# Model-wide activations stored 320 words per row instead of 322, and MLP inner chunks begun at shifted addresses

## The chip, the cores and the metric

The kernel runs on one core of a Trainium2 chip. The metric is the time of one execution in device microseconds (us), as the median of the runs shown. The core's engines are named as the profile names them: PE is TensorE, which multiplies; PEld is the same engine's weight load; DVE is VectorE, ACT is ScalarE, POOL is GpSimd and SP is SyncE, which here only issues transfers. SBUF is the on-chip memory of 128 partitions in which operands lie; PSUM is the memory into which TensorE writes.

## The reference, cut to what matters

One inference step of a two-layer decoder over 320 tokens (256 of a prompt, 8 sequences of 8 new tokens), model width 2048, all in float32:

```python
# layer 0: gated linear attention; layer 1: chunked spatial gating; after each a dense MLP
h = mixer(x)                                           # x @ w_in, the mixer itself, ... @ w_out
x = layer_norm(ALPHA * x + h)
x = layer_norm(ALPHA * x + square(relu(x @ w1)) @ w2)  # w1: 2048 x 8192, w2: 8192 x 2048
```

Nearly all of the arithmetic is the products with the weights: w_in and w_out of both mixers, w1 and w2 of both layers.

## The kernel before

**Layout.** Activations lie transposed: features on the 128 partitions, tokens on the free axis. A model-wide activation has 2048 features, so it is 16 "k rows" of 320 tokens side by side in each partition. The kernel keeps every such activation as two float32r tiles, a high part and a low part, whose sum is the float32 value; the weights are split in the same way as they arrive. Four buffers hold all these activations in turn: a0 and a1 (high and low), b0 and b1. Each has 16 rows of TW = 322 words: 320 tokens, and two columns that are used only where a layer norm's gain and offset ride along in the product. So row k begins 1288 * k bytes behind the start of its buffer. As the program is built, the buffers begin at byte 18976 (a0), 39584 (a1), 60192 (b0) and 150176 (b1) of a partition, which is 32, 160, 32 and 160 modulo 256.

**Products.** `group` (L143) works out two feature tiles of 128 outputs. It fetches the weights in units of 4 k rows by 256 columns (`unit`, L117: the transfer is issued by SP at L127, ACT rounds to the high part at L128, DVE takes the low part at L129), and for each k row and each of the two output tiles `mm3` (L136) issues three matmuls of 320 columns: low weights by high activation (L139), high weights by low activation (L140), high by high (L141). In the names of the profile `mm<-hh,wl` is: into the PSUM tile mm, moving operand hh (the activation), stationary operand wl (the weights). The activation's name is x (input), o (mixer output of layer 0), dg (an unnormed activation times the gain, with the two extra columns: 322 wide), y (normed), h (inner chunk of the MLP) or p (mixer output of layer 1), followed by h or l for its part. The weight units rotate through rings of SBUF tiles; in a partition all tiles of one ring begin at 160 modulo 256 (ring a, the only one during the heads), all tiles of the other at 224 (ring b).

```python
    def mm3(ps, wh, wl, kk, n, rh, rl, k, c0, cn, first, last):
        s = slice(n * P, (n + 1) * P)
        x_h, x_l = rh[:, k, c0 : c0 + cn], rl[:, k, c0 : c0 + cn]
        nc.tensor.matmul(ps, wl[:, kk, s], x_h, start=first, stop=False)
        nc.tensor.matmul(ps, wh[:, kk, s], x_l, start=False, stop=False)
        nc.tensor.matmul(ps, wh[:, kk, s], x_h, start=False, stop=last)
...
    def bigtile(tag, dt, name):
        return (lp if tag == "b1" else big).tile([P, KT, TW], dt, tag=tag, name=nm(name))

    def parts(pair, name):
        return bigtile(pair + "0", F32R, name + "h"), bigtile(pair + "1", F32R, name + "l")
```

**Stages.** In order of time: the four heads of layer 0 (products with x, in buffers a, between which small matmuls of the attention run); the output product with o (buffers a); the MLP of layer 0, whose y lies in a and whose inner chunks h lie in b: for each of four chunks c of 2048 inner features `mlp` (L774) makes h = square(relu(y @ w1)) and adds h @ w2 to the residual z; then layer 1: y in b for the spatial gating, p in b, and the second MLP with y in b and h in a. The first two pairs of output tiles after a norm run on dg instead of y (`gemm_of`, L741). The last layer norm ends the program. There are 736 weight units, so 17,664 matmuls of the lines L139 to L141, of which 576 are 322 columns wide and the rest 320.

**What sets the order.** Each engine runs its own stream in the order in which the program was built; transfers of weights are issued ahead as ring tiles come free.

Of the kernel before, what the change touches and what calls it, by code (L numbers as in the profile page):

```python
# [15 lines left out]
P = 128  # L16
D = 2048
KT = D // P          # feature tiles of a model-width activation
TP = 256             # prompt tokens
DB, DS = 8, 8        # sample batch and new tokens  # L20
T = TP + DB * DS     # tokens side by side on the free axis
TW = T + 2           # with two columns for the gain and the offset of a norm
H = 4
DK, DV = 256, 512
CH = 64              # GLA chunk
# [5 lines left out]
UK = 4               # k tiles in a weight unit  # L31
UN = 256             # columns in a weight unit
NU = KT // UK

# columns of the per-feature vectors
# [6 lines left out]
class Ring:  # L42
    """Where the split weight units of a GEMM live."""
# [5 lines left out]
class Side:  # L49
    """Work beside a GEMM, handed out in steps over the weight units still to come."""  # L50
# [16 lines left out]
def step_kernel(ctx: ExitStack, tc: tile.TileContext, A):  # L67
# [7 lines left out]
    # ------------------------------------------------------------ pools  # L75
# [13 lines left out]

    def mmtile(n=T):  # L90
        """Of the banks for products; two more of them once the heads are done."""
        if mx is not None:
            banks[0] = (banks[0] + 1) % 6
        return (mx if banks[0] > 3 else mm).tile([P, n], F32, tag="mm", name=nm("mm"), padded_shape=[P, 512])
# [4 lines left out]
    # ------------------------------------------------------------ constants  # L99
# [16 lines left out]
    # ------------------------------------------------------------ weights  # L116
    def unit(w, row0, q, col0, ring):  # L117
        """UK k tiles of UN columns, as exact high and low parts."""
        raw = wraw.tile([P, UK, UN], F32, tag="raw", name=nm("raw"))
        src = w[row0 // (UK * P) + q, col0 // UN]  # L120
        hi = ring.pool.tile([P, UK, UN], F32R, tag="h" + ring.tag, name=nm("wh"))
        lo = ring.pool.tile([P, UK, UN], F32R, tag="l" + ring.tag, name=nm("wl"))
        units[0] += 1
        step = 2 if units[0] <= 2 else UK  # the first ones in parts, for an early start
        for k in range(0, UK, step):
            ks = slice(k, k + step)
            nc.sync.dma_start(raw[:, ks, :], src[:, ks, :])  # L127
            nc.scalar.copy(hi[:, ks, :], raw[:, ks, :])  # L128
            nc.vector.tensor_sub(lo[:, ks, :], raw[:, ks, :], hi[:, ks, :].bitcast(F32))  # L129
        return hi, lo  # L130
# [11 lines left out]

    def group(w, row0, cols, rh, rl, evict, side=None, width=T, before=None):  # L143
        """Two feature tiles of w[row0:row0+D].T @ x for each of cols, k tiles outermost in units."""
        ps = [mmtile(width) for _ in range(2 * len(cols))]
        for q in range(NU):
            if before is not None:
                before(q)
            for i, c in enumerate(cols):
                wh, wl = unit(w, row0, q, c, next_ring())  # L150
                for n in range(2):
                    for kk in range(UK):
                        k = q * UK + kk
                        mm3(ps[2 * i + n][:], wh, wl, kk, n, rh, rl, k, 0, width, k == 0, k == KT - 1)
                if side is not None:
                    side()
        for n in range(2 * len(cols)):
            evict(n, ps[n])

    def rsqrt(out, src, scale, eps, eps_t, pool):  # L160
        """1 / sqrt(scale * src + eps): the table's value and a Newton step."""
# [10 lines left out]
    # ------------------------------------------------------------ layer 0: GLA  # L172
# [3 lines left out]
    def bigtile(tag, dt, name):  # L176
        """A model-wide activation in one of four buffers; b1 comes with the later pool."""
        return (lp if tag == "b1" else big).tile([P, KT, TW], dt, tag=tag, name=nm(name))

    def parts(pair, name):  # L180
        return bigtile(pair + "0", F32R, name + "h"), bigtile(pair + "1", F32R, name + "l")
# [9 lines left out]
    # x, by k tiles, and its parts  # L191
    xT = A["xT"].rearrange("(k p) t -> p k t", p=P)
    def load_x(q):
        """x for quarter q of the features."""
# [12 lines left out]
    # causal masks: prompt [s of a 128-block, (t | t of the second block)]; sample [(i, part, s), (i', t)]  # L207
# [20 lines left out]
    # where the masked scores and the sample's queries go; what they leave is zero  # L228
# [9 lines left out]
    # per head: [1, d1, d1 d2 | 1, d2] for the queries, [d1 d2 d3, d2 d3, d3, 1] for the keys  # L238
# [8 lines left out]
    def load_gates():  # L247
        """The gate's weights; the second ones by 32 rows: high parts (twice), low parts."""
# [7 lines left out]
    def low_gate():  # L256
        """rows 0-15 x @ w_hi, rows 16-31 x @ w_lo, [hi | lo] side by side in the stationary operand; three times"""
# [22 lines left out]
    def bc4(ap):  # L280
        """[P, 64] sample columns -> [P, 8, 4, 8], the same for each part."""
        return ap.rearrange("p (b o t) -> p b o t", b=DB, o=1)
# [4 lines left out]
    class Head:  # L287
        """The gates of a head, its k, q and v, and what GLA reads of them."""
# [16 lines left out]
        def gate_logits(hd):  # L305
            """exp(-|z|) and min(z, 0) of the logits z; a step for each table of ScalarE."""
# [12 lines left out]
        def gate_sums(hd):  # L319
            """log_sigmoid(z) = min(z, 0) - ln(1 + exp(-|z|)), summed along the chunks."""  # L320
# [93 lines left out]
        def project_kq(hd, side, before=None):  # L414
            """k and q together, as all four tiles of the other heads' work beside it are there."""
# [25 lines left out]
        def weigh(hd):  # L441
            """o * g * silu(r)"""
# [5 lines left out]
        def finish(hd):  # L448
            """... over the root of the mean square"""
# [4 lines left out]
        def prompt_scores(hd):  # L454
            """Scores of all chunk pairs at once, [s, t] for each block of 128 keys."""
# [64 lines left out]
        def sample_first(hd):  # L520
            """rows: 64 of the queries' high parts, 64 of the low ones"""
# [7 lines left out]
        def sample_step(hd, b, kt):  # L529
            """What state tile (b, kt) adds to o, and its update."""  # L530
# [39 lines left out]
        def steps(hd):  # L570
            """GLA, by steps: the prompt at once, the sample's sequences one by one."""
# [22 lines left out]
    # ------------------------------------------------------------ the rest: residual stream z  # L594
# [7 lines left out]
    def second_half():  # L602
        """The heads are done: their tiles make room for the residual stream."""
# [16 lines left out]
    class Norm:  # L620
        """LayerNorm over the features of src, of sums of d = src - c, c[t] the mean of the first half.

        The GEMM that reads it starts on d * g: with the columns g and offset beside it, its rows are
        put right by mean and 1/std as they leave.
        """

        def __init__(self, src, vg, vb, raw=None, last=False):
# [5 lines left out]
            if raw is not None:  # L633
                self.raw = gh, gl_ = parts(raw, "dg")
# [12 lines left out]
        def total(self, x):  # L647
            """Sums over the partitions, of x in its two parts."""
# [9 lines left out]
        def take(self, j):  # L658
            """The shifted tile j into the sums; where nothing follows, the last one straight into the totals."""
# [19 lines left out]
        def add(self, j):  # L679
            """Tile j is there; of the second half already shifted."""  # L680
# [9 lines left out]
            else:  # L690
                # any c does, as long as it is the same everywhere
# [9 lines left out]
        def close(self):  # L701
            """The mean (negative) and 1/std."""
# [8 lines left out]
        def apply(self, j, yh=None, yl=None):  # L711
            """In place (x - mean) * rstd * g + b of one feature tile, and its parts."""
# [10 lines left out]
        def correct(self, ps):  # L723
            """From a row tile of w.T @ [d * g | g | b]: the product with the norm, less its offset, and that."""
# [7 lines left out]
    def gemm(w, row0, col0, rh, rl, evict, quad=False, side=None, before=None):  # L732
        """All feature tiles, in pairs; the first two pairs together where x is only coming."""
# [7 lines left out]
    def gemm_of(norm, out, w, col0, evict_raw, evict):  # L741
        """w.T @ norm(x): its first tiles from d * g while the norm itself is worked out."""
        yh, yl = parts(out, "y")
# [8 lines left out]
    def residual_gemm(w, rh, rl, row0, scale, vg, vb, raw, quad=False, side=None, before=None, last=False):  # L752
        """z <- scale * z + x @ w, shifted, with the sums for its norm along with the evictions."""
# [20 lines left out]
    def mlp(i, norm, y_in, h_in, vg, vb, raw, last=False):  # L774
        """z, normed, and its MLP; z and the sums for the norm of what comes out."""
        w1, w2 = A["mlp_w1"][i], A["mlp_w2"][i]
        NC_ = 4
        for c in range(NC_):
            hs = []

            def sq_relu(j, x, r):
                if not hs:
                    hs.extend(parts(h_in, "h"))
# [17 lines left out]
            if c == 0:  # L801
                yh, yl = gemm_of(norm, y_in, w1, 0, evict_raw, evict)
# [9 lines left out]
    # layer 0: mixer output, norm, MLP, norm; the last head is still at work beside the first product  # L812
# [10 lines left out]
    # ------------------------------------------------------------ layer 1: spatial gating  # L823
    nv = v = wsT = bb = wss = u_st = None

    def spatial():
        """Causal spatial weights, transposed: [s, g, t]; of the sample the first rows, block-diagonal."""
        nonlocal wsT, bb, wss, u_st
        bsp = bigtile("a1", F32, "bsp")
        bs = bsp[:].rearrange("p k t -> p (k t)")  # L830
# [38 lines left out]
    def mix(j):  # L869
        """The normed feature tile j, mixed over its tokens."""  # L870
# [15 lines left out]
    def mixed(j, pm, g):  # L886
        """... with the bias; in v once its rows are out."""
# [33 lines left out]
    # the last norm, over three engines: d - mean on TensorE from the parts of both, or all of it on GpSimd  # L921
# [101 lines left out]
```

## Time and profile before

| | |
|---|---|
| median of 3 runs | 2784.06 us (2784.03 to 2784.24) |
| profiled execution, from its first to its last instruction (span) | 2783.4 us |
| TensorE: matmul busy, weight load busy | 2763.0 us (99%), 2714.9 us (98%) |
| VectorE, ScalarE, GpSimd busy | 1543.0 us (55%), 1179.7 us (42%), 52.6 us (2%) |
| matmuls recorded | 18,493 |

The span is that of one execution; the median stands 0.7 us above it. Busy time of TensorE counts matmuls that overlap (each is pipelined behind the one before), so 99% says that it nearly always has one under way, not that it could not be quicker.

### The profile page before, as it was taken

The page shows a single profiled execution, that of the slowest core. Times are in us where ns is not written, and L with a number is a line of the kernel's source. Part 1 is how long each engine was busy: PE and PEld are TensorE (multiplying, and loading weights), DVE is VectorE, ACT ScalarE, POOL GpSimd, SP SyncE. Part 2 cuts the span into 40 slices and gives each one's busy share as a digit, 9 for nine tenths or more (in the row PEclk, how much of TensorE's full clock was granted, in tenths as well). Part 3 has the DMA queues.
Part 4 walks back from the last instruction along what each step waited for, and adds up shares of the span by engine and source line. Part 5 has one row for each costly group of instructions (what it writes and reads, how often), then busy time and mean ns, then how long its engine had stood idle before and what let it go on. Part 6 is the DMA issues. An engine that isn't in the chain of part 4 may idle for free.

```text
span 2783.4 us, 44616 instructions
## 1 busy us (share of the span) xinstructions
PE 2763.0 (99%) x18493; PEld 2714.9 (98%) x18493; DVE 1543.0 (55%) x2276; ACT 1179.7 (42%) x1698; POOL 52.6 (2%) x83
## 2 busy tenths in 40 slices
PE   8999999999999999999999999999999999999998
PEld 8898998999999999999999999999999999999998
DVE  6566566886444444444468764587444444444446
ACT  5545454555334324323435553455324323423433
POOL 1000000000000000000000000000000000000001
PEclk9999999999999999999999999999999999999999
DMA  6556565654444445444445444445444444444442
GB/s 221 167 190 227 152 212 190 208 156 152 148 149 152 147 149 151 147 149 151 148 137 175 149 136 126 148 144 152 150 147 151 150 147 151 150 146 151 150 147 75
DMA packets 126396, 434.52 MB, mean 156 GB/s; under 512 B 13681, under 2 KB 17905, under 8 KB 126193
## 3 DMA queue, kind: packets, MB, share of 16 engines
q1 hardware_dynamic: 118800, 407.29, 47.3%
q0 software_dynamic: 6512, 23.20, 2.4%
q8 instruction: 144, 2.36, 0.3%
q10 hardware_dynamic: 880, 1.18, 0.1%
q14 instruction: 60, 0.48, 0.1%
HBM read 409.60 MB, written 22.02 MB: 155 GB/s over the span
## 4 chain that ended last, share of the span: by engine, by line
PE 98%; DVE 0%; ACT 0%; DMA 0%; issue 0%; SPq 0%; ACTq 0%; DVEq 0%
PE mm L139 31%; PE mm L141 31%; PE mm L140 31%; PE gl L540 1%; PE gl L543 1%; PE gl L498 1%; DMA xr<-xT 0%; PE gl L882 0%; PE gl L482 0%; PE gl L883 0%; ACT z L956 0%; DMA raw<-gla_w_in 0%; PE gl L874 0%; PE gl L483 0%; PE gl L409 0%
## 5 line engine op out<-in xcount | busy, mean ns | idle before, releaser
L129 DVE TENSOR_TENSOR wl<-raw,wh 128x1024 fp32r<-128x1024 f32 (+1 forms) x738 | 900.5, 1221 | 991.5 <-ACT wh L128 988.9
L128 ACT CAST wh<-raw 128x1024 fp32r<-128x1024 f32 (+1 forms) x738 | 771.4, 1046 | 1258.3 <-PE mm L141 1140.6
L141 PE MATMUL mm<-yh,wh 128*128 128x320 f32 x2368 | 734.0, 310 | 0.0
L140 PE MATMUL mm<-yl,wh 128*128 128x320 f32 x2368 | 732.4, 310 | 0.0
L139 PE MATMUL mm<-yh,wl 128*128 128x320 f32 x2368 | 727.8, 310 | 0.0
L141 PE MATMUL mm<-hh,wh 128*128 128x320 f32 x2048 | 635.3, 310 | 0.0
L139 PE MATMUL mm<-hh,wl 128*128 128x320 f32 x2048 | 634.4, 310 | 0.0
L140 PE MATMUL mm<-hl,wh 128*128 128x320 f32 x2048 | 633.6, 309 | 0.0
L140 PEld LDWEIGHTS mm<-yl,wh 128*128 128x128 f32 x2368 | 447.0, 189 | 0.2
L141 PEld LDWEIGHTS mm<-yh,wh 128*128 128x128 f32 x2368 | 446.1, 188 | 0.1
L139 PEld LDWEIGHTS mm<-yh,wl 128*128 128x128 f32 x2368 | 444.5, 188 | 0.0
L140 PEld LDWEIGHTS mm<-hl,wh 128*128 128x128 f32 x2048 | 386.7, 189 | 0.0
L141 PEld LDWEIGHTS mm<-hh,wh 128*128 128x128 f32 x2048 | 385.8, 188 | 0.0
L139 PEld LDWEIGHTS mm<-hh,wl 128*128 128x128 f32 x2048 | 385.8, 188 | 0.0
L139 PE MATMUL mm<-xh,wl 128*128 128x320 f32 x768 | 246.4, 321 | 9.7 <-ACT xh L200 5.8
L140 PE MATMUL mm<-xl,wh 128*128 128x320 f32 x768 | 241.1, 314 | 0.2 <-DVE xl L201 0.2
L141 PE MATMUL mm<-xh,wh 128*128 128x320 f32 x768 | 240.2, 313 | 0.0
L139 PEld LDWEIGHTS mm<-xh,wl 128*128 128x128 f32 x768 | 145.7, 190 | 22.1 <-issue 10.8
L140 PEld LDWEIGHTS mm<-xl,wh 128*128 128x128 f32 x768 | 146.3, 190 | 2.8 <-issue 1.4
L141 PEld LDWEIGHTS mm<-xh,wh 128*128 128x128 f32 x768 | 146.0, 190 | 2.2 <-issue 1.2
L792 ACT ACTIVATE r<-mm 128x320 f32<-128x320 f32 x120 | 52.6, 439 | 64.5 <-PE mm L141 64.5
L139 PE MATMUL mm<-ph,wl 128*128 128x320 f32 x256 | 78.9, 310 | 1.0 <-ACT ph L915 1.0
(272 smaller groups left out, 2493.5 us busy)
## 6 DMA issues: line engine op xcount, KB each, us to landing
raw<-mlp_w SPq DMA_DIRECT2D x512, 512.0 KB, 3.5
raw<-gla_w_in SPq DMA_DIRECT2D x94, 512.0 KB, 4.1
raw<-sg_w_in SPq DMA_DIRECT2D x64, 512.0 KB, 3.5
st<-state SPq DMA_DIRECT2D x32, 512.0 KB, 3.9
o_state_s<-st POOLq DMA_DIRECT2D x32, 512.0 KB, 3.8
raw<-gla_w_out SPq DMA_DIRECT2D x32, 512.0 KB, 4.3
raw<-sg_w_out SPq DMA_DIRECT2D x32, 512.0 KB, 3.6
z<-xT POOLq DMA_DIRECT2D x2, 1280.0 KB, 11.4
```

The lines of the kernel that those rows point to most:

```text
L128: nc.scalar.copy(hi[:, ks, :], raw[:, ks, :])
L129: nc.vector.tensor_sub(lo[:, ks, :], raw[:, ks, :], hi[:, ks, :].bitcast(F32))
L139: nc.tensor.matmul(ps, wl[:, kk, s], x_h, start=first, stop=False)
L140: nc.tensor.matmul(ps, wh[:, kk, s], x_l, start=False, stop=False)
L141: nc.tensor.matmul(ps, wh[:, kk, s], x_h, start=False, stop=last)
L498: nc.tensor.matmul(pu[:], hd.ktp[:, blk, kt * P : (kt + 1) * P], hd.vtp[:, blk, :], start=(blk == 0), stop=(blk == 1))
L540: nc.tensor.matmul(po[:], qm[:, kt, b * P : (b + 1) * P], part[:], start=False, stop=(b == DB - 1 and kt == 1 and part is sth))
L543: nc.tensor.matmul(pu[:], hd.kts[32 * i : 32 * (i + 1), g, kt * P : (kt + 1) * P], hd.vts[32 * i : 32 * (i + 1), g, :], start=True, stop=True)
L792: nc.scalar.activation(r[:], ps[:], AF.Relu)
```

## The change

Each buffer becomes one flat run of 16 * 322 words of the same size at the same place. An activation is now a piece of it with rows of 320 words (1280 bytes, which is 5 * 256), beginning at a start offset in words; only the dg activations and the tile of the spatial weights keep rows of 322. Start offsets are 0 except: the inner chunks h of layer 0 begin at 8 * c words (32 * c bytes) in both buffers; those of layer 1 begin at 0 in the high part's buffer and 8 * c in the low part's; the high part of y of layer 1's MLP begins at word 32 (128 bytes). Besides this the diff only drops comments, which shifts no line of the products (L117 to L158) and moves later ones by a line or two.

```diff
-    def bigtile(tag, dt, name):
-        """A model-wide activation in one of four buffers; b1 comes with the later pool."""
-        return (lp if tag == "b1" else big).tile([P, KT, TW], dt, tag=tag, name=nm(name))
-
-    def parts(pair, name):
-        return bigtile(pair + "0", F32R, name + "h"), bigtile(pair + "1", F32R, name + "l")
+    def bigtile(tag, dt, name, width=T, start=0):
+
+        t = (lp if tag == "b1" else big).tile([P, KT * TW], dt, tag=tag, name=nm(name))
+        return t[:, start : start + KT * width].rearrange("p (k t) -> p k t", t=width)
+
+    def parts(pair, name, width=T, starts=(0, 0)):
+        return (bigtile(pair + "0", F32R, name + "h", width, starts[0]),
+                bigtile(pair + "1", F32R, name + "l", width, starts[1]))
...
-                self.raw = gh, gl_ = parts(raw, "dg")
+                self.raw = gh, gl_ = parts(raw, "dg", TW)
...
-    def gemm_of(norm, out, w, col0, evict_raw, evict):
-        """w.T @ norm(x): its first tiles from d * g while the norm itself is worked out."""
-        yh, yl = parts(out, "y")
+    def gemm_of(norm, out, w, col0, evict_raw, evict, starts=(0, 0)):
+
+        yh, yl = parts(out, "y", starts=starts)
...
-                    hs.extend(parts(h_in, "h"))
+                    hs.extend(parts(h_in, "h", starts=(8 * c, 8 * c) if i == 0 else (0, 8 * c)))
...
-                yh, yl = gemm_of(norm, y_in, w1, 0, evict_raw, evict)
+                yh, yl = gemm_of(norm, y_in, w1, 0, evict_raw, evict, starts=(0, 0) if i == 0 else (32, 0))
...
-        bsp = bigtile("a1", F32, "bsp")
-        bs = bsp[:].rearrange("p k t -> p (k t)")
+        bs = bigtile("a1", F32, "bsp", TW).rearrange("p k t -> p (k t)")
```

As built, every engine has the same instructions in the same order with the same waits, and every tile lies where it lay. What differs is the address at which an activation's rows are written and read, and that 16 instructions at the start (the split of x, two k rows at a time) now write one run of 640 words instead of two of 320.

Where the rows begin, in bytes modulo 256, before and after (matmuls of 320 columns, the high part serving two of three):

| activation | matmuls | before: high, low | after: high, low |
|---|---|---|---|
| x, o, p, y of layer 0's MLP and of the gating, h of chunk 0 of both layers | 9,600 | 32 to 152, 160 to 24, in steps of 8 with k | 32, 160 |
| h of layer 0, chunks 1, 2, 3 | 768 each | the same | 64, 192; 96, 224; 128, 0 |
| y of layer 1's MLP | 2,880 | the same | 160, 160 |
| h of layer 1, chunks 1, 2, 3 | 768 each | the same | 32, 192; 32, 224; 32, 0 |

## Rows read from the trace of the kernel before

**Rows 1.** The page: the span, and busy time, share of the span and instructions of each engine.

```profile
span 2783.4 us, 44616 instructions
...
PE 2763.0 (99%) x18493; PEld 2714.9 (98%) x18493; DVE 1543.0 (55%) x2276; ACT 1179.7 (42%) x1698; POOL 52.6 (2%) x83
```

**Rows 2.** The page: the granted clock of TensorE in 40 slices of the span (tenths of full speed), and the chain of work that ended last, its shares by engine and by line.

```profile
PEclk9999999999999999999999999999999999999999
...
PE 98%; DVE 0%; ACT 0%; DMA 0%; issue 0%; SPq 0%; ACTq 0%; DVEq 0%
PE mm L139 31%; PE mm L141 31%; PE mm L140 31%; PE gl L540 1%; PE gl L543 1%; PE gl L498 1%; DMA xr<-xT 0%; PE gl L882 0%; PE gl L482 0%; PE gl L883 0%; ACT z L956 0%; DMA raw<-gla_w_in 0%; PE gl L874 0%; PE gl L483 0%; PE gl L409 0%
```

**Rows 3.** The waits of TensorE's matmuls: line, what it waited for, us in total, times, longest.

```profile
PE mm L139 <- ACT xh L200: 5.8, 1, 5.8
PE mm L139 <- DVE qd L386: 2.1, 1, 2.1
...
PE mm L140 <- DVE xl L201: 0.2, 1, 0.2
```

**Rows 4.** Busy time by stretches of the span, TensorE alone. [...] The stretches: layer 0's h of chunk 0, y of chunk 1, h of chunk 1; layer 1's h of chunks 0 and 2; the last norm.

```profile
core 0: us, PE busy (x), PEclk, DMA share, GB/s
...
700.50:813.70 113.20, 113.20 (x770) 1.00 0.49 149
813.70:926.90 113.20, 113.20 (x770) 1.00 0.49 149
926.90:1040.20 113.30, 113.30 (x770) 1.00 0.49 149
...
1970.30:2083.60 113.30, 113.30 (x771) 1.00 0.49 149
...
2196.80:2310.00 113.20, 113.20 (x770) 1.00 0.49 149
...
2763.60:2783.40 19.80, 10.54 (x62) 0.94 0.38 133
```

**Rows 5.** The timeline of TensorE in layer 0's MLP, h in buffers b: start in us, duration in us, engine, line, operation. Of each three matmuls of a k row only the first (L139) is shown: k rows 11 of the second output tile, then 12, 13, 14, 15 and 12 of the next unit's tiles.

```profile
738.98 0.31 PE L139 MATMUL mm<-hh,wl 128*128 128x320 f32 x1
...
739.44 0.32 PE L139 MATMUL mm<-hh,wl 128*128 128x320 f32 x1
...
739.89 0.30 PE L139 MATMUL mm<-hh,wl 128*128 128x320 f32 x1
...
740.33 0.31 PE L139 MATMUL mm<-hh,wl 128*128 128x320 f32 x1
...
740.76 0.31 PE L139 MATMUL mm<-hh,wl 128*128 128x320 f32 x1
...
741.21 0.31 PE L139 MATMUL mm<-hh,wl 128*128 128x320 f32 x1
```

**Rows 6.** The same place of a group in layer 1's MLP, h in buffers a (the first row is again k row 11), and the weight load that begins beside that first matmul.

```profile
2008.80 0.31 PE L139 MATMUL mm<-hh,wl 128*128 128x320 f32 x1
2008.80 0.19 PEld L140 LDWEIGHTS mm<-hl,wh 128*128 128x128 f32 x1
...
2009.26 0.32 PE L139 MATMUL mm<-hh,wl 128*128 128x320 f32 x1
...
2009.71 0.30 PE L139 MATMUL mm<-hh,wl 128*128 128x320 f32 x1
...
2010.15 0.31 PE L139 MATMUL mm<-hh,wl 128*128 128x320 f32 x1
```

**Rows 7.** The timeline of TensorE: the first and the last of the matmuls counted in the prediction's averages. By time: first of all 16,774 and of the 8,388 whose row begins on a multiple of 16 bytes (9.66); first of the 8,386 whose row begins 8 bytes past one (10.26); first of the rows at 32 modulo 64, and at 160 modulo 256 (13.15); first at 32 modulo 256 (13.30); first at 0 modulo 64 (17.41); then the last ones: at 160 modulo 256 (2750.82), at 32 modulo 256 (2750.96), at 32 modulo 64 (2758.61), at 0 modulo 64 (2762.18), on a multiple of 16 bytes (2763.05), and of all and 8 bytes past a multiple of 16 (2763.35).

```profile
9.66 0.31 PE L139 MATMUL mm<-xh,wl 128*128 128x320 f32 x1
...
10.26 0.31 PE L139 MATMUL mm<-xh,wl 128*128 128x320 f32 x1
...
13.15 0.31 PE L140 MATMUL mm<-xl,wh 128*128 128x320 f32 x1
...
13.30 0.31 PE L141 MATMUL mm<-xh,wh 128*128 128x320 f32 x1
...
17.41 0.31 PE L140 MATMUL mm<-xl,wh 128*128 128x320 f32 x1
...
2750.82 0.31 PE L140 MATMUL mm<-hl,wh 128*128 128x320 f32 x1
...
2750.96 0.31 PE L141 MATMUL mm<-hh,wh 128*128 128x320 f32 x1
...
2758.61 0.31 PE L141 MATMUL mm<-hh,wh 128*128 128x320 f32 x1
...
2762.18 0.31 PE L141 MATMUL mm<-hh,wh 128*128 128x320 f32 x1
...
2763.05 0.31 PE L141 MATMUL mm<-hh,wh 128*128 128x320 f32 x1
...
2763.35 0.31 PE L140 MATMUL mm<-hl,wh 128*128 128x320 f32 x1
```

**Rows 8.** The split of x by two k rows at a time: duration of one in ns (least, median, most), first and last start, shapes.

```profile
L200 ACT CAST xh<-xr x8: 727/728/732, 5.0 to 19.8; 128x640 fp32r<-128x640 f32 x8
...
L201 DVE TENSOR_TENSOR xl<-xr,xh x8: 819/824/1104, 5.8 to 21.7; 128x640 fp32r<-128x640 f32 x8
```

## The prediction, made before the changed kernel was run

> **What bounds the kernel now.** First the page's busy times: TensorE has a matmul under way for 2763.0 of 2783.4 us, the other engines are far from full [rows 1]. Then the chain that ended last: 98% of it is TensorE, 93% the three product lines L139 to L141 [rows 2], and TensorE's longest wait for another engine is 5.8 us, once, at the start [rows 3]. [...] So the time is the number of matmuls times the time from the start of one to the start of the next; I call this the step. A faster ACT, DVE or transfer would be worth nothing.
>
> Next the step itself. The inner stages of both MLPs have 768 matmuls each, whichever buffers they read and whatever goes on beside them, and each takes 113.2 to 113.3 us [rows 4]: 113.25 / 768 = 147.5 ns. [...]
>
> The timeline shows that the step is not even. From one k row's L139 to the next takes three steps: in [rows 5] 0.46, 0.45, 0.44, 0.43, 0.45 us. In the other layer, other buffers, the same place gives 0.46, 0.45, 0.44 us again [rows 6]. The records have whole nanoseconds, so I averaged steps over all matmuls of 320 columns with a product matmul directly behind and no stall (a step of at most 170 ns): 16,774 of them, mean 147.41 ns, standard deviation 2.9, first and last in [rows 7]. Sorted by line, row start modulo 256 and weight address, outside the heads, the same class repeats to 1.1 ns, while the classes' means run from 141 to 157 ns. The step is therefore set by where a matmul reads, or by its place in the sequence; in this kernel those two go together, as k row 3 always begins at the same bytes modulo 256.
>
> Two sortings speak for the address. By row start modulo 64, the means run from 146.4 to 148.5 ns; worked out for the heads alone (one weight ring, attention matmuls between) and for all the rest, the eight means agree with a correlation of 0.8. And buffers a and b, whose starts agree modulo 256 and in little else, give the same step [rows 4].
>
> **The change part by part.** The order of all engines and the waits stay, so every term is a change of the step.
>
> *Rows 320 words apart.* Before, a product sweeps 16 row starts in steps of 8 bytes and pays their mean. After, all 16 rows begin at the same bytes modulo 256, so a stage pays what its one or two starts cost. Of the 17,088 matmuls of 320 columns, 15,040 then begin at 32 modulo 64: the 9,600 with starts 32 and 160; the second chunk of layer 0 shifted by 64 bytes (768); y of layer 1's MLP (2,880); the high parts of layer 1's chunks 1 to 3 (1,536) and one of their low parts (256). The other 2,048 begin at 0 modulo 64. The trace of before has both: 2,086 matmuls at 32 modulo 64 with a mean of 146.62 ns, 2,096 at 0 modulo 64 with 148.08 ns (first and last of each in [rows 7]). So 15,040 x (146.62 - 147.41) = -11.9 us and 2,048 x (148.08 - 147.41) = +1.4 us: -10.5 us.
>
> A finer sorting, modulo 256, has fewer samples: starts at 32 (always a high part) 148.02 ns over 687 matmuls, at 160 (always a low part) 144.58 ns over 346 [rows 7]. The 9,600 with two high and one low take (2 x 148.02 + 144.58) / 3 = 146.87 ns, -0.54 ns, -5.2 us. If it is the address alone, layer 1's y, all at 160, takes 144.58 ns: 2,880 x -2.83 = -8.2 us; if it is the part, nothing. The remaining 4,608, with their starts priced in the same way, come to +0.6 us. Sum -12.7 us, or -4.5 us without the gain on y. I take -12 us, between the two full sums.
>
> *The shifted starts* are in these sums: chunk 3 of layer 0 (128 and 0) is the dear one, at 0 modulo 64; the others lie near the mean or below.
>
> *Alignment.* All rows after begin on a multiple of 16 bytes, before every second one. In the trace the 8,388 aligned ones have a mean of 147.08 ns and the 8,386 others 147.73 [rows 7].
> [...]
>
> *Weight loads.* The load for the next matmul begins as the matmul begins (2008.80 in both rows of [rows 6]), so both read SBUF at once. [...]
> [...]
>
> *The rest.* The 576 matmuls of 322 columns keep their rows. Writes by ACT and DVE go to other addresses; they are hidden behind 99% of TensorE. The 16 merged instructions of the split of x take 728 and 824 ns at the median [rows 8]; only the first lie ahead of the first products, and if a run of 640 cost or saved a tenth, that would be 0.15 us. The last norm's 19.8 us [rows 4] stay.
>
> The profiled execution's 2783.4 us less 12 us are 2771.4; the median stands 0.7 us above its span, so 2772 us, -0.43%. What a measurement of this kernel can tell from no change is about 0.2%, 5.6 us.
>
> **The bounds.** The unknown is the step where the same row start follows itself 16 times, which before never happens. From the dearest and the cheapest three steps of the timeline, 457 ns (0.46 in [rows 5]) and 436 ns (0.43), a step of one start could be 152.3 or 145.3 ns: 17,088 x +4.9 = +84 us or 17,088 x -2.1 = -36 us, if every stage fell on the same end. There are eight different pairs of starts, the commonest with 56% of the matmuls, so I count half of the upper end at most.
>
> **The rivals.**
> *Faster by more.* If the step's unevenness is a phase between two reads, equal rows let it settle, and it settles where nothing collides: the step of rows at 160, 144.58 ns, for all: 17,088 x -2.83 = -48 us, 2736 us; for half of the stages 2760. For it: classes repeat to 1.1 ns, so the pattern does lock. Against: nothing says that it locks at the good end.
>
> *Slower.* The same mechanism, locked at the bad end. Before, the sweep averages good and bad starts; after, 9,600 matmuls share one pair. If these settle at the 150.20 ns that rows at 128 modulo 256 have now (698 matmuls within the same first and last), they cost 9,600 x 2.79 = +27 us: 2811 us. It decides as soon as their step passes 147.41 + 5.6 us / 9,600 = 148.0 ns, where the high parts at 32 modulo 256 already stand by themselves. Against it: their low parts are the cheapest rows there are.
>
> *No change.* The step depends on the place in the sequence and not on the address, or starts average out over the weights' addresses: 2784 us. For it: place and address can't be parted in this trace, and all stages have one step [rows 4]. Against: the sorting by row start agrees between the heads and the rest.
> [...]
>
> [...]
>
> **How the numbers follow.** The forecast, in which averages by row start carry over, 0.42 (own range 2763 to 2778); faster by more 0.18; slower 0.20; no change 0.12; only the lines 0.08. Faster by over 0.2% is the first two, 0.60; the last two make 0.20 for no difference; slower 0.20. The range leaves out about a tenth at each side: 2740, most of the way to the locked good end, to 2795, halfway to the locked bad one.
>
> **What would show it.** Right: stages of 768 matmuls no longer take one time; those with starts 32 and 160 take 112.8 us (146.9 ns), layer 0's chunk 3 longer than its chunk 1, layer 1's y less than layer 0's; within a stage the three steps of every k row are alike. Wrong if every stage still takes 113.25 us (place, not address), if the stages at 32 and 160 take over 113.7 us (locked badly), or if all fall below 112 us. The dg products, whose rows don't move, must keep their time whatever happens; if they change too, something else did it.

## The result, and the profile after

The changed kernel takes 2770.79 us (median of 4 runs, 2770.2 to 2770.9) against 2784.15 us: a ratio of 0.995, 95% interval 0.9936 to 0.9964. That is 13.4 us or 0.48% faster; forecast were 12 us and 2772 us. Its profiled execution has a span of 2769.1 us, 14.3 us below that of [rows 1]. One run of a kernel further down, the one without shifts, took 3334.01 us at a granted clock of 0.753; no figure below uses it.

The page after, the lines that answer to [rows 1] and [rows 2]: span, busy times, granted clock, the chain by line.

```profile
span 2769.1 us, 44616 instructions
...
PE 2749.8 (99%) x18493; PEld 2701.6 (98%) x18493; DVE 1542.8 (56%) x2276; ACT 1179.4 (43%) x1698; POOL 52.8 (2%) x83
...
PEclk9999999999999999999999999999999999999999
...
PE mm L139 31%; PE mm L141 31%; PE mm L140 31%; PE gl L542 1%; PE gl L545 1%; PE gl L500 1%; DMA xr<-xT 0%; PE gl L883 0%; PE gl L484 0%; PE gl L884 0%; ACT z L957 0%; DMA raw<-gla_w_in 0%; PE gl L875 0%; PE gl L485 0%; PE gl L409 0%
```

Nothing moved but TensorE's own pace: the same instructions, the same granted clock (0.999 of full speed over the span, before and after), the same chain, DVE and ACT busy as long as before. PE is shorter by 13.2 us.

Busy time of TensorE by stages, as in [rows 4] (stretch in us from the span's start, its length, busy us and matmuls that touch it, of which up to two at the edges belong to the neighbours, granted clock as a share of full speed, DMA share, GB/s). The stretches are layer 0's h of chunks 0 to 3, one of the dg products with unmoved rows, then layer 1's h of chunks 1 and 2.

```profile
697.97:810.50 112.53, 112.53 (x770) 1.00 0.50 150
923.04:1035.99 112.95, 112.95 (x771) 1.00 0.48 150
1148.52:1260.95 112.43, 112.43 (x771) 1.00 0.48 150
1373.47:1485.98 112.51, 112.51 (x772) 1.00 0.50 150
...
1485.98:1515.03 29.05, 29.05 (x198) 1.00 0.48 146
...
2186.04:2298.05 112.01, 112.01 (x771) 1.00 0.48 151
2410.68:2523.44 112.76, 112.76 (x771) 1.00 0.49 150
```

Before, all of these h stages took 113.2 to 113.3 us. Now each has its own time, by where its rows begin, and all are shorter. The dg product kept its time (29.04 us in the trace before, from 1493.24 to 1522.28).

The timeline at the place of [rows 5] (k row 11 onwards, the first of each three matmuls):

```profile
736.21 0.31 PE L139 MATMUL mm<-hh,wl 128*128 128x320 f32 x1
...
736.65 0.31 PE L139 MATMUL mm<-hh,wl 128*128 128x320 f32 x1
...
737.09 0.31 PE L139 MATMUL mm<-hh,wl 128*128 128x320 f32 x1
...
737.52 0.31 PE L139 MATMUL mm<-hh,wl 128*128 128x320 f32 x1
...
737.97 0.31 PE L139 MATMUL mm<-hh,wl 128*128 128x320 f32 x1
```

From one k row to the next it is 0.44, 0.44, 0.43, 0.45 us where it was 0.46, 0.45, 0.44, 0.43. Averaged as in the prediction, the step (start of one matmul to the start of the next) is 146.54 ns over 16,765 matmuls, standard deviation 2.0, where it was 147.41 and 2.9. 17,088 x 0.87 = 14.9 us: the step alone accounts for the gain (13.4 us in the medians, 14.3 us in the spans).

### The profile page after: what moved, and what is told of

It reads as the page before. It is cut to its first block, busy times and chain, and to the rows that moved or that the text cites. A ratio compares the mean times of both kernels' runs of the same rounds, so it can differ in the third digit from the quotient of the medians.

```text
span 2769.1 us, 44616 instructions
## 1 busy us (share of the span) xinstructions
PE 2749.8 (99%) x18493; PEld 2701.6 (98%) x18493; DVE 1542.8 (56%) x2276; ACT 1179.4 (43%) x1698; POOL 52.8 (2%) x83
## 4 chain that ended last, share of the span: by engine, by line
PE 98%; ACT 1%; DVE 0%; DMA 0%; issue 0%; SPq 0%; ACTq 0%; DVEq 0%
PE mm L139 31%; PE mm L141 31%; PE mm L140 31%; PE gl L542 1%; PE gl L545 1%; PE gl L500 1%; DMA xr<-xT 0%; PE gl L883 0%; PE gl L484 0%; PE gl L884 0%; ACT z L957 0%; DMA raw<-gla_w_in 0%; PE gl L875 0%; PE gl L485 0%; PE gl L409 0%
## 5 line engine op out<-in xcount | busy, mean ns | idle before, releaser
L141 PE MATMUL mm<-yh,wh 128*128 128x320 f32 x2368 | 731.3, 309 | 0.0
L140 PE MATMUL mm<-yl,wh 128*128 128x320 f32 x2368 | 728.7, 308 | 0.0
L139 PE MATMUL mm<-yh,wl 128*128 128x320 f32 x2368 | 724.7, 309 | 0.0
L141 PE MATMUL mm<-hh,wh 128*128 128x320 f32 x2048 | 632.1, 309 | 0.0
L139 PE MATMUL mm<-hh,wl 128*128 128x320 f32 x2048 | 631.8, 308 | 0.0
L140 PE MATMUL mm<-hl,wh 128*128 128x320 f32 x2048 | 631.4, 308 | 0.0
L140 PEld LDWEIGHTS mm<-yl,wh 128*128 128x128 f32 x2368 | 444.7, 188 | 0.2
L141 PEld LDWEIGHTS mm<-yh,wh 128*128 128x128 f32 x2368 | 444.0, 187 | 0.1
L139 PEld LDWEIGHTS mm<-yh,wl 128*128 128x128 f32 x2368 | 443.0, 188 | 0.0
L139 PEld LDWEIGHTS mm<-hh,wl 128*128 128x128 f32 x2048 | 385.0, 188 | 0.0
L140 PEld LDWEIGHTS mm<-hl,wh 128*128 128x128 f32 x2048 | 384.5, 188 | 0.0
L141 PEld LDWEIGHTS mm<-hh,wh 128*128 128x128 f32 x2048 | 384.3, 188 | 0.0
L139 PE MATMUL mm<-xh,wl 128*128 128x320 f32 x768 | 245.7, 320 | 8.6 <-ACT xh L202 5.8
L140 PE MATMUL mm<-xl,wh 128*128 128x320 f32 x768 | 241.3, 314 | 0.2 <-DVE xl L203 0.2
L141 PE MATMUL mm<-xh,wh 128*128 128x320 f32 x768 | 239.7, 312 | 0.0
L139 PEld LDWEIGHTS mm<-xh,wl 128*128 128x128 f32 x768 | 145.8, 190 | 21.2 <-issue 10.9
L140 PEld LDWEIGHTS mm<-xl,wh 128*128 128x128 f32 x768 | 146.1, 190 | 2.8 <-issue 1.4
L141 PEld LDWEIGHTS mm<-xh,wh 128*128 128x128 f32 x768 | 145.9, 190 | 2.3 <-issue 1.2
L139 PE MATMUL mm<-ph,wl 128*128 128x320 f32 x256 | 78.6, 309 | 1.0 <-ACT ph L916 1.0
```

## The experiments

Steps below are such averages over a stage, from the records of its trace. "Pair" means the start offsets of high and low part in words (4 bytes); offset 0 is byte 32 modulo 256 in the high part's buffer and 160 in the low part's, both multiples of 16. "Line" is a name for 16 bytes of a partition that begin at a multiple of 16, not a unit that a trace shows: 320 columns that begin on one lie in 80 of them, those that begin 4, 8 or 12 bytes past one in 81.

**What carries the gain: the shifted starts, equal rows, or whole 16-byte lines?** Three kernels, each against the changed one:

Without any shift, every row of both parts on a whole line:

```diff
-                    hs.extend(parts(h_in, "h", starts=(8 * c, 8 * c) if i == 0 else (0, 8 * c)))
+                    hs.extend(parts(h_in, "h", starts=(0, 0)))
...
-                yh, yl = gemm_of(norm, y_in, w1, 0, evict_raw, evict, starts=(0, 0) if i == 0 else (32, 0))
+                yh, yl = gemm_of(norm, y_in, w1, 0, evict_raw, evict, starts=(0, 0))
```

> All activations keep rows of 320 words, but every start offset is 0, so that every stage reads rows at 32 (high part) and 160 (low part) modulo 256. If the row start alone sets the step, every stage of 768 matmuls now takes the same time, the one that chunk 0 takes in the changed kernel, 112.5 us (146.5 ns a matmul), and the whole is within 3 us of the changed kernel (2771 us). If the shifted starts carried the gain, the time goes back towards 2784 us. If the place in the sequence counted and not the address, the chunks would still differ from each other as they do in the changed kernel (145.8 to 147.1 ns).

Every row 8 bytes past a line (dg keeps its rows): the same two calls with (2, 2), the same default in `gemm_of`, and

```diff
-    def parts(pair, name, width=T, starts=(0, 0)):
+    def parts(pair, name, width=T, starts=(2, 2)):
```

> Rows of 320 words, every start offset 2 words (8 bytes): all rows of the large products begin at 40 and 168 modulo 256, 8 bytes past a multiple of 16, and all rows of a stage still begin at the same bytes. If the gain comes from beginning on a multiple of 16 bytes, it is lost or turned round: a step of 147.7 ns or more, 2789 us. If it comes from all rows beginning alike, whatever the bytes, the step is near 146.5 ns and the time near 2771 us.

Rows of 324 words: the two calls with (0, 0), and

```diff
+TR = T + 4
...
-    def bigtile(tag, dt, name, width=T, start=0):
+    def bigtile(tag, dt, name, width=TR, start=0):
...
-        t = (lp if tag == "b1" else big).tile([P, KT * TW], dt, tag=tag, name=nm(name))
+        t = (lp if tag == "b1" else big).tile([P, KT * TW + 64], dt, tag=tag, name=nm(name))
...
-    def parts(pair, name, width=T, starts=(0, 0)):
+    def parts(pair, name, width=TR, starts=(0, 0)):
```

> Rows of 324 words (1296 bytes), start offset 0, buffers 256 bytes longer so that all of them and the weight rings begin where they did modulo 256. Every row begins on a multiple of 16 bytes, but the 16 rows of a product sweep through 16 different starts again, in steps of 16 bytes. If beginning on a multiple of 16 bytes is what counts, the step is at or below 147.1 ns, as in the aligned rows of the kernel before, and the time is 2771 to 2778 us. If all rows must begin alike, the step is 147.4 ns and the time 2784 us.

Measured: 2769.96 us, ratio to the kernel before (2784.74 us beside it) 0.9946 (0.9929 to 0.9962); 2808.86 us, 1.0085 (1.0068 to 1.0102); 2776.31 us, 0.9969 (0.9956 to 0.9982). TensorE in h stages of layer 0, first without shifts (chunks 0, 1), then 8 bytes past a line (0, 1), then with rows of 324 (0, 1):

```profile
698.50:811.02 112.52, 112.52 (x770) 1.00 0.48 150
923.57:1036.09 112.52, 112.52 (x770) 1.00 0.49 150
```

```profile
703.68:818.02 114.34, 114.34 (x770) 1.00 0.48 148
932.37:1046.71 114.34, 114.34 (x770) 1.00 0.49 148
```

```profile
696.66:809.51 112.85, 112.85 (x770) 1.00 0.48 150
922.37:1035.22 112.85, 112.85 (x770) 1.00 0.48 150
```

Without shifts all stages take one time again, that of chunk 0 of the changed kernel (146.53 ns), so the address sets the step and not the place in the program; and the shifts are worth nothing in sum (spans 2769.4 us without and 2769.1 us with them). Equal rows that begin 8 bytes past a line are dearer than the sweep of the kernel before: 148.9 ns. Sweeping rows that all begin on a line take 146.9 ns. In medians, whole lines alone give 2784.74 - 2776.31 = 8.4 us and equal rows another 2776.31 - 2769.96 = 6.4 us; by the steps of the whole kernels (147.41, 146.87 and 146.52 ns, times 17,088) it is 9.2 and 6.0 us.

**Does the weights' address matter?** Ring a moved by 64 bytes, nothing else modulo 256:

```diff
+    pad1 = ctx.enter_context(tc.tile_pool(name="pad1", bufs=1))
+    nc.vector.memset(pad1.tile([P, 16], F32, tag="pad1", name="pad1")[:], 0.0)
     wa = ctx.enter_context(tc.tile_pool(name="wa", bufs=4))
+    pad2 = ctx.enter_context(tc.tile_pool(name="pad2", bufs=1))
+    nc.vector.memset(pad2.tile([P, 48], F32, tag="pad2", name="pad2")[:], 0.0)
```

> The changed kernel with ring a of the weights moved by 64 bytes (a pad of 64 bytes before it, 192 behind it), so that both rings begin at 224 modulo 256; all activations stay where they are modulo 256. If the step is set by where the activation's row and the weights lie to each other, the units of ring a take the steps that those of ring b have in the changed kernel: in the stages at 32 and 160 the matmuls on the low part go from 146.7 to 143.3 ns, the mean of the stage from 146.5 to 146.2 ns, and the whole gets about 4 us faster. If the weights' address doesn't matter, and the difference between the units of the two rings comes from something else, every stage keeps its time.

Measured: 2772.19 us, 0.9953 (0.9938 to 0.9968), the same as the changed kernel within the intervals. Layer 0's h of chunks 0, 1, 2 and layer 1's of chunk 1:

```profile
696.73:809.36 112.63, 112.63 (x770) 1.00 0.48 150
922.01:1034.64 112.63, 112.63 (x770) 1.00 0.49 150
1147.28:1259.91 112.63, 112.63 (x770) 1.00 0.49 150
...
2185.99:2297.78 111.79, 111.79 (x771) 1.00 0.49 151
```

Half of the expectation came true: in layer 0's chunk 0 the low part's matmuls of ring a went from 146.7 to 143.3 ns, as in ring b. So the weights' address does shape the single step. But the high part's rose (147.3 to 148.3 ns over both rings), and the mean went to 146.67 and not to 146.2. Stages that differed by up to 0.8 ns now share 146.67 ns; only the pair 0, 8 stands out, with 145.56. How a stage's sum can be held while its parts move, these runs don't explain.

**Does the step follow the columns of the activation, or the length of the weight load beside the matmul?** Other widths of the activation or of the weights in single stages:

```diff
+        if wide is not None and (wide > T or k > 0):
+            a = min(k, KT - 2) * T if wide > T else k * T
+            x_h, x_l = (r.rearrange("p k t -> p (k t)")[:, a : a + wide] for r in (rh, rl))
+            ps = ps[:, 0:wide]
+        if narrow is not None and k > 0:
+            m = slice(n * P, n * P + narrow)
+            nc.tensor.matmul(ps[0:narrow], wl[:, kk, m], x_h, start=first, stop=False)
+            nc.tensor.matmul(ps[0:narrow], wh[:, kk, m], x_l, start=False, stop=False)
+            nc.tensor.matmul(ps, wh[:, kk, s], x_h, start=False, stop=last)
+            return
...
+                gemm(w1, 0, c * D, yh, yl, evict, wide=(None, 512, 384, 256)[c] if i == 0 else None,
+                     narrow=(None, 64, 32, 96)[c] if i == 1 else None)
```

> All start offsets 0, rows of 320 words. Six stages leave the reference: the first products (y by w1) of the inner chunks 1, 2 and 3 read 512, 384 and 256 columns instead of 320 in layer 0 (the extra ones from the rows behind, dropped at the eviction), and in layer 1 load only 64, 32 and 96 columns of the weights in the lines L139 and L140 (so part of the outputs lacks its low parts); k row 0 keeps all its columns. [...] Theory A, a rate of the activation's read: 146.67 / 80 = 1.833 ns for each 16-byte line, so 234.7, 176.0 and 117.3 ns for 512, 384 and 256 columns (128, 96, 64 lines), and the width of the weights changes nothing. [...]

768 matmuls each with 512, 384 and 256 columns of the activation, then with 64, 32 and 96 columns of the weights in L139 and L140:

```profile
810.56:987.22 176.66, 176.66 (x770) 1.00 0.32 99
1099.75:1234.46 134.71, 134.71 (x770) 1.00 0.41 126
1347.03:1439.10 92.07, 92.07 (x771) 1.00 0.59 183
2139.00:2251.80 112.80, 112.80 (x772) 1.00 0.49 150
2364.10:2476.20 112.10, 112.10 (x771) 1.00 0.48 151
2588.80:2701.00 112.20, 112.20 (x769) 1.00 0.50 150
```

Steps of 230.0, 175.4 and 118.1 ns (256 without k row 0): theory A wanted 234.7, 176.0, 117.3. It doesn't hold: the step is not in proportion to the lines; from 256 to 512 columns a column costs 0.437 ns, with some 6 ns a matmul left (an estimate: 118.1 - 256 x 0.437). Nor does the length of the weight load set the step: the narrow weights' loads did shorten, from 188 ns to 134, 108 and 161 ns, and the matmuls beside them (L139 and L141, without k row 0) have steps of 146.9, 145.3 and 146.4 ns. With a quarter of the weights' columns beside it the matmul saved 1.3 ns (against 146.5 ns), with half of them nothing.

**Which pairs are good?** Two kernels with other starts in every stage, all on whole lines; the edit is the `starts` of each call of `parts` and `gemm_of`.

> Rows of 320 words, other start offsets in every stage, all multiples of 16 bytes. In words (high part, low part): x 0 and 8; o 16 and 16; y of layer 0's MLP 24 and 32; its h in chunks 0 to 3: 4, 8; 8, 16; 16, 24; 4, 12; y of the gating 4, 4; p 0, 4; y of layer 1's MLP 0, 8; its h 24, 0; 8, 0; 16, 8; 0, 32. If beginning on a 16-byte line is nearly all that counts, all stages lie between 146 and 147.1 ns. If the distance from the high to the low part's start matters, the stages with a low part 160 bytes behind (0, 8; 8, 16; 16, 24; 24, 32; 4, 12) share the 145.6 to 145.8 ns that layer 1's chunk 1 has in the changed kernel. If it is the pair with the weights' start, only 0, 8 has it.

> As the run before, with other starts: x 0 and 16; o 32 and 32; y of layer 0's MLP 12 and 20; its h 0, 12; 0, 20; 0, 28; 4, 0; y of the gating 16, 0; p 8, 20; y of layer 1's MLP 32 and 8; its h 12, 0; 20, 0; 28, 0; 8, 12. If beginning on a 16-byte line is nearly all that counts, all stages lie between 146 and 147.1 ns; if single pairs are much better or worse, they show here, down to 142 or up to 150 ns.

In the second kernel two starts are the other way round than the expectation says: y of the gating is at 32, 8 and layer 1's y at 16, 0. One run each: 2764.18 and 2772.96 us, beside 2785.22 of the kernel before. Layer 0's h of chunk 0 in the first (4, 8), layer 1's y of chunk 1 in the second (16, 0):

```profile
694.45:807.61 113.16, 113.16 (x771) 1.00 0.48 149
```

```profile
2073.87:2186.91 113.04, 113.04 (x770) 1.00 0.48 149
```

The pairs lie between 145.8 ns (32, 8 and 0, 8) and 147.35 ns (4, 8; 16, 0 took 147.2). That is wider at both ends than the 146 to 147.1 ns expected: all are below the 148.9 ns of rows 8 bytes past a line, but among whole lines the pair still decides about 1.5 ns, more than the 0.87 ns that the change gained. Low parts 160 bytes behind their high parts (a distance of 8 words) took 145.8 to 146.4 ns in the first of the two kernels, but 12, 20 in the second took 147.0: the distance by itself is no rule. Which property of a pair makes it good these runs don't tell. Then the pair 0, 8 in every stage, alone and with ring a moved as above:

> Rows of 320 words, and in every stage the high part's rows begin at 0 and the low part's at 8 words (32 and 192 modulo 256). Stages with this pair had steps of 145.8 to 145.9 ns in three kernels so far (x, layer 1's y and a chunk of layer 1), against a mean of 146.5 in the changed kernel. If the step follows the pair of starts, all stages take 145.9 ns and the whole 17,088 x 0.65 = 11 us less than the changed kernel, 2760 us. If it was the stage and not the pair, the time stays at 2771 us.

> The same with ring a of the weights moved by 64 bytes, as in the run that moved it before. There the stage with this pair took 145.57 ns, all other aligned stages 146.66. If that carries over to all stages, the whole takes 17,088 x 0.97 = 17 us less than the changed kernel, 2754 us; if the pair alone counts, it equals the run without the moved ring.

Measured: 2759.46 us, ratio 0.9909 (0.9893 to 0.9926), and 2755.15 us, 0.9895 (0.9881 to 0.991). Layer 0's h of chunk 0 in the one and in the other:

```profile
695.79:807.79 112.00, 112.00 (x771) 1.00 0.48 151
```

```profile
694.99:806.78 111.79, 111.79 (x771) 1.00 0.49 151
```

Expected were 2760 and 2754 us. The second, 145.55 ns in nearly all stages, is the fastest kernel of this study, 15.6 us ahead of the changed one.

**Is it the number of lines that a row touches?** Starts off a line in one part or both, and other column counts:

> Rows of 320 words with start offsets that are not all multiples of 16 bytes. In words (high, low): h of layer 0's chunks 0 to 3: 0, 2; 2, 0; 1, 1; 1, 0; h of layer 1's: 0, 1; 3, 3; 6, 6; 2, 10; y of layer 1's MLP 10, 2; o 0, 2; the rest 0, 0. If each matmul pays for the 16-byte lines that its own row touches, 80 or 81, whatever the bytes past a line's start, a stage with both parts off costs 148.3 to 148.9 ns, one with only the low part off a third of the difference to 146.5 (147.1 to 147.3), one with only the high part off two thirds (147.7 to 148.1). If 8 bytes past a line is special, the stages at 1 and 3 words stay at 146.5 ns or go elsewhere.

> All start offsets 0. The first products of the inner chunks 1, 2, 3 read 316, 318 and 322 columns in layer 0 and 324, 326 and 312 in layer 1 instead of 320 (missing ones leave outputs out, extra ones are dropped); k row 0 keeps at least 320. From an aligned start these touch 79, 80, 81 and 81, 82, 78 lines of 16 bytes. If the step goes by lines, 318 columns take what 320 take (146.5 ns) and 322 what 324 take, with 1.7 to 1.8 ns from line to line. [...]

In the first kernel it is y of the gating that is at 0, 2, and o at 0, 0. It took 2785.58 us; h of layer 0 with pairs 0, 2; 2, 0; 1, 1; 1, 0; then of layer 1 with 3, 3 and 6, 6:

```profile
698.10:810.96 112.86, 112.86 (x771) 1.00 0.47 150
923.49:1037.46 113.97, 113.97 (x771) 1.00 0.48 148
1149.99:1265.45 115.46, 115.46 (x770) 1.00 0.47 147
1377.99:1492.10 114.11, 114.11 (x771) 1.00 0.48 148
2195.45:2306.87 111.42, 111.42 (x771) 1.00 0.47 151
2420.65:2535.47 114.82, 114.82 (x771) 1.00 0.48 147
```

One part 8 bytes off costs less than both, as expected, the low part (146.95 ns) less than the high one (148.4 ns, above the 147.7 to 148.1 expected). But the third and fifth rows break the count of lines: a row that begins 4, 8 or 12 bytes past a line touches 81 lines each time, and with both parts there took 150.3, 148.2 to 149.5, and 145.1 ns. The column counts broke it too. First products with 316, 318, 322, 324, 326 and 312 columns (k row 0 keeps 320 in the narrower ones):

```profile
808.84:919.88 111.04, 111.04 (x770) 1.00 0.49 152
1032.41:1144.29 111.88, 111.88 (x770) 1.00 0.48 151
1256.84:1371.01 114.17, 114.17 (x770) 1.00 0.49 148
2071.05:2185.46 114.41, 114.41 (x771) 1.00 0.48 148
2297.99:2413.97 115.98, 115.98 (x770) 1.00 0.48 146
2526.51:2636.58 110.07, 110.07 (x770) 1.00 0.47 153
```

Without k row 0 in the narrower ones, the steps are 144.5, 145.6, 148.7, 149.0, 151.0 and 143.1 ns, with 146.5 for 320. Above 320 the step goes by lines (2.1, 0.3, 2.0 ns), below it by columns (318 is 0.9 ns below 320, with the same 80 lines).

The quick start 12 bytes past a line, in nearly every stage:

> Rows of 320 words that begin 12 bytes past a multiple of 16 in nearly every stage, after the one stage at 3 and 3 words took 145.1 ns in the run before although its rows touch 81 lines. In words (high, low): x 3 and 3; o 7 and 7; y of layer 0's MLP 3 and 11; its h 11, 11; 3, 7; 7, 3; 15, 15; y of the gating 3, 3; p 3, 0; y of layer 1's MLP 3, 3; its h 0, 3; 3, 19; 19, 3; 23, 31. If 12 bytes past a line is quick by itself, all stages with both parts there lie at 144.5 to 145.7 ns, the two mixed ones between that and 146.5, and the whole takes about 17,088 x 1.4 = 24 us less than the changed kernel, 2747 us. If the lines touched are what counts and that one stage was a lucky pair, the others go to 148.3 to 149 ns and the whole to about 2800 us.

Here o is at 3, 3 and y of the gating at 7, 7. Measured: 2758.76 us, 0.9906 (0.9892 to 0.992). Layer 0's h of chunk 0 (pair 11, 11), layer 1's of chunk 0 (0, 3):

```profile
691.97:803.65 111.68, 111.68 (x770) 1.00 0.46 151
1949.79:2063.61 113.82, 113.82 (x771) 1.00 0.45 148
```

It is quick by itself: 145.06 ns in x and o, 145.09 in layer 1's y and 145.16 in y of the gating, whose two parts have one offset in words, 145.4 to 145.5 ns in the two other stages of that kind (11, 11 and 15, 15), and 145.8 to 146.5 ns in the pairs 12 bytes past a line with two different offsets; nowhere 148. So the 2747 us expected were missed: the pairs with different offsets, layer 0's y (3, 11) among them, took back some 8 us by their steps. Mixing a part 12 bytes past with one on a line is dear (0, 3: 148.2; 3, 0: 147.05 ns), some 4 us more. Starts 3, 3 in every stage were not run.

## Why the prediction was right, and where its steps were not

**The bound** was read rightly: the step of the product matmuls is the time, and the change of the step accounts for all of the gain, at one granted clock (0.999). The rival "no change" fell on both counts: the address counts, since stages part as soon as their addresses do and meet again without shifts; and starts don't average out.

**The sums** (-10.5 and -12.7 us, taken as -12; measured -13.4 in the medians, -14.3 in the spans) were right in size by luck, through errors that offset each other.

- Starts 32 and 160: 146.87 ns expected, 146.53 measured; -8.4 us instead of -5.2. These 9,600 matmuls carried more than half of the gain; the finer sum had given them 5.2 us of 12.7.
- Layer 1's y at 160 and 160: 144.58 ns if the address alone counted, 147.4 if the part did; measured 146.66, so -2.2 us instead of -8.2. The low parts at 160 did not owe their 144.58 ns to their own address alone; the moved ring, with 143.3 ns for the low and 148.3 for the high at unmoved rows, points the same way.
- The other six pairs: +0.6 us expected, -4.2 us measured. Chunk 3 of layer 0 (128 and 0), forecast as the dear one at about 149 ns, took 146.30; layer 1's chunk 1 (32 and 192), forecast at 147.7, is the best of the changed kernel, 145.83. The trace before already had the answer: of the matmuls on the rows at 128, whose 150.20 ns were the price, the first of three (L139, behind a row off the line) took 152.3 ns and the third (L141, behind a row on it) 148.2 ns. One start had two prices, by what stood around it. The reason given for chunk 3, a start at 0 modulo 64, held for chunk 1 (64 and 192) as well.

Of the signs named, the stages parted and those at 32 and 160 took 112.5 us (112.8 forecast), while the dg products kept theirs; but chunk 3 of layer 0 was shorter than chunk 1 (112.51 and 112.95 us), layer 1's y dearer than layer 0's (146.66 and 146.53 ns), and the steps stayed uneven: by line, k row, output tile and ring, the means in layer 0's chunk 0 run from 141.6 to 151.6 ns, from 140.8 to 158.3 before.

So the step of the argument that failed is "a stage pays what its starts cost": the average by row start modulo 64 or 256 doesn't carry over to single stages. What carries over is whether rows begin on a 16-byte line or 8 bytes past it (146.5 and 148.9 ns where all rows of a stage begin alike). By the averages of the trace before, where aligned and other rows alternate, it was worth 17,088 x (147.08 - 147.41) = -5.6 us by itself, the case "only the lines" of the forecast's chances; run alone it gives 8.4 us in the medians, 9.2 by the steps. The alternation had blurred it: aligned rows of the kernel before took 147.08 ns, sweeping aligned rows by themselves 146.9. The other 6 us came with all rows alike, at a pair of starts that happens to lie in the middle of those tried (146.5 of 145.8 to 147.35 ns). A count of lines would have given it the right sign, 80 against 81, but doesn't give the 145.1 ns of rows 12 bytes past, which lie in 81 as well.

**The rivals.** "Slower", the step locked at a bad end, is real, but at another address than the one named: 8 bytes past a line it costs 24 us, and a single stage at 4 bytes past took 150.3 ns. What spoke against it, that the low parts at 160 modulo 256 are the cheapest rows there are, misread the trace: rows at 16 modulo 256 took 142.7 ns. "Faster by more" is real as well: 2755 us, with one pair in all stages and both rings alike.

**A collision of the two reads**, the activation's and the next weights', which the rivals "faster by more" and "slower" assume, was the author's guess and is not shown. The weights' address shifts single steps by 3 ns (the low part's in ring a from 146.7 to 143.3), which fits it, but the stage's mean by only 0.1 ns (146.53 to 146.67); and a weight load of 108 ns instead of 188 saved at most 1.3 ns of 146.5.

The work said to be hidden stayed hidden, and the start and the end kept their times: TensorE's longest wait for another engine is again 5.8 us, for the split of x, and the last norm takes 19.9 us where it took 19.8.

## What to carry to other kernels

Where matmuls of float32r stand back to back, as here at a granted clock of 0.999, look at the byte at which each k row of the moving operand begins, and keep it the same within 16 bytes for all rows, on a line if nothing better has been measured: all rows 8 bytes past a line were 1.6% dearer a matmul than all on it (148.9 against 146.5 ns), and a row stride of two words more than a multiple of four, which puts every second row there, cost 0.4% on average (147.41 against 146.87 ns). Averages by address from a sweep did not give the price of one address, and for layer 0's chunk 3 not even its direction; one kernel with another start in each stage measures a dozen pairs at once.

## What the runs showed of the hardware that was not expected

- With high and low part at one offset within 16 bytes, the step of 320 columns was 145.8 to 147.35 ns on the line (145.56 with both rings at one offset), 150.3 ns 4 bytes past (one stage), 148.2 to 149.5 ns 8 bytes past, 145.1 to 146.5 ns 12 bytes past. Why 12 is quick and 4 slow stays open.
- Over 256, 384 and 512 columns of float32r, one stage each, the step rose by 0.437 ns a column from end to end (118.1, 175.4 and 230.0 ns), with some 6 ns a matmul besides, an estimate from these; next weights of 64 columns instead of 128 didn't shorten it (146.9 against 146.5 ns at 320 columns).
- With both weight rings at one offset modulo 256, the stages on whole lines, whose means had lain between 146.3 and 147.1 ns, took 146.66 to 146.68 ns each in the MLPs, but for one pair at 145.56 ns. What singles that pair out was not found.
